# Reordering the FFN products of a hybrid GLA/Fourier block: activations turned among the A products, w_d granules moved, adaLN steps moved

## The chip, the cores and the metric

The kernel runs on one core of a Trainium2 chip. The metric is device time in microseconds (us) of one launch; lower is better. A core has five engines with queues of their own: TensorE (PE in the profile; its weight loads are PEld), VectorE (DVE), ScalarE (ACT), GpSimd (POOL) and SyncE (SP, which here only issues DMAs). Each works through its own queue in order; semaphores make one wait for another. TensorE writes into PSUM, which has eight banks; VectorE and ScalarE read from there.

## The reference, cut to what matters

One layer of a backbone is computed for 128 context tokens and 256 latent tokens, 384 in all, with d_model 2048. The mixing half of the layer (gated linear attention, Fourier branch, gates, output projection) is not touched. What the change touches is the channel half:

```
mod = silu(cond) @ w_ada + b_ada           # six vectors of 2048: shift, scale, gate, twice
h   = rmsnorm(x, norm_pre_ffn) * (1 + sc2) + sh2
ff  = (silu(h @ w_ffn_gate) * (h @ w_ffn_up)) @ w_ffn_down
x   = x + ga2 * rmsnorm(ff, norm_post_ffn)
```

The hidden width is 5632. All arithmetic is float32 in accuracy: each operand is split into a high part (rounded to fp32r) and a low part (the rest), and a product takes three matmuls, high by high, low by high and high by low.

## The kernel before, in words

**Chunks and granules.** The hidden width is cut into NFC = 11 chunks of 512 columns (`FC` = 4 blocks of 128). Chunk 0 is computed plainly. From chunk c = 1 on, chunk c's gate and up products and the down product of chunk c - 1 are interleaved; one such stretch is called stage c here. The weights come in granules of 128 x 1024 float32 (512 KB). A step of the hand-written list `steps` consumes one granule.

**Saved products.** The three 128-token tiles, the halves of the contraction and the gate/up pair are treated with a Strassen-like scheme, so that some products use sums of weights and sums of activations. The kinds of a stage's steps, four steps (i = 0 to 3) of each:

- A (12 matmuls a step), B (12), C (12), E (6), F (6), G (12), H (6): the gate and up products of chunk c. A, B, C and G use loaded granules; the granules of B, E, F and H are formed on VectorE by subtracting others (lines L1412, L1436, L1437, L1439: 128 x 1024 each).
- D with i = 4 to 7 (18 matmuls each): w_d's plain granules, columns 1024 to 2047 of the output, for chunk c - 1. An even i opens three PSUM tiles (`pd_tiles`, pool psm, tag mm), an odd i closes them.
- DA to DH (6 or 12 matmuls): w_d's block products, columns 0 to 1023, by the saving scheme. They use the turned activations (`hid`) and sums of them (`dt["S"]`).

Matmuls of all these have the line L1530 in the profile; the tile name tells them apart: pgu for A to H, pdn for D, pds for DA to DH.

**Splitting.** `grab2` (called at the start of a step) takes the step's split granule, lets loads be issued (`load_more`) and splits the granule three steps ahead (`split_next`): ScalarE copies the high part (L1429, whi), VectorE subtracts to get the low part (L1440, wlo). There are four buffers for each part. Between the two, `split_next` emits up to three operations of the list `pend`, and then the weight sums that this granule needs.

**Turning.** The hidden activations of three token tiles lie as g0, g1, s5 (tokens in rows) and are needed with hidden columns in rows. `turn_hid` makes four transposes on TensorE into a psm bank (tile ptr, L1594) and appends the ScalarE copy and the VectorE subtraction (L1596) to `pend`. In the kernel before this happens after B0, B1 and B2. After B3, `hid_sums` appends seven operations that form `dt["S"]`: they read tiles t = 1 and t = 2 straight out of PSUM (L1604 on ScalarE, two operations at L1605 and two at L1606 on VectorE), and then split the result (L1607). A D step with even i first empties `pend`. The psm pool has three banks, which ptr, pdn, pds and the small reductions share.

**Evictions.** `evict` appends to `pend` what combines the PSUM results at the end of A to H: after E and F an addition and a SiLU, after G two additions and two products (L1583, L1584), after H a product (L1587).

**The last adaLN vector.** ga2 is computed on the side by the generator `ada_last`: 64 steps, each loading 256 KB of w_ada (tile w, two buffers) and running two VectorE operations (L1473; L1471 for the first step of a quarter); after each 16 a small reduction on TensorE (pr, ptm) and three small VectorE operations. `step(ada)` runs it at a rate: before 0.85 per call, called after each A step, each G step, and each D step with i of 4 or more.

**The last stage.** In stage 10 (`LAST` = 10) the down product of chunk 9 is all plain (D0 to D7), and after H follow the rest of them and, after a turn into `hidE`, the eight plain granules of chunk 10.

**Sums in HBM.** Down products of chunks 0 to 8 are staged by ScalarE (`to_sums`, L1632) and added into an HBM array by DMAs from POOL's queue (L1636); the last stage reads them back (`sums_back`, `sums_rest`).

The queues of TensorE, ScalarE, VectorE and GpSimd run in the order in which the code emits (`manual_schedule`); SP's loads are placed by the framework.

Of the kernel before, what the change touches and what calls it, by code (L numbers as in the profile page):

```python
# [96 lines left out]
def tile_step(ctx: ExitStack, tc: tile.TileContext, a, o):  # L97
# [152 lines left out]
    def step(side):  # L250
        if side is not None:
            next(side, None)
# [792 lines left out]
    with ExitStack() as s:  # L1045
# [292 lines left out]
        steps = []  # L1338
        LAST = NFC - 1
        for c in range(1, NFC):  # L1340
            steps += [("A", c, i) for i in range(4)] + [("B", c, i) for i in range(4)]
            if c < LAST:
                dd = iter([("D", c - 1, 4), ("D", c - 1, 5), ("DA", c - 1, 0), ("DB", c - 1, 0), ("DC", c - 1, 0),
                           ("D", c - 1, 6), ("D", c - 1, 7)] + [("D" + k, c - 1, 0) for k in "EFGH"])
            else:
                dd = iter([("D", c - 1, i) for i in range(4)] + [None, ("D", c - 1, 4), None, ("D", c - 1, 5)])
            more = lambda: [x for x in (next(dd, None),) if x]
            for i in range(4):
                steps += [("C", c, i), ("E", c, i)] + more()
            for i in range(4):  # L1350
                steps += [("F", c, i), ("G", c, i)] + more()
            for i in range(4):
                steps += [("H", c, i)] + more()
        steps += [("D", NFC - 2, 6 + i) for i in range(2)]
        d_order = (0, 2, 1, 3)
        steps += [("D", NFC - 1, 2 * n + k) for n in d_order for k in range(2)]

# [281 lines left out]
        def sums_back():  # L1639

            psums.append(actp.tile([P, 6, 512], F32, tag="B_hi", name="psums"))
            w = [adap.tile([P, 2, 512], F32, tag="adaw", name="back", bufs=2) for _ in range(2)]
            at = dict(q2=unit(0, 0), q3=unit(0, 1), p2=unit(1, 0), p3=unit(1, 1), p4=unit(2, 0), p5=unit(2, 1))
            at.update({k: w[n // 2][:, n % 2, :] for n, k in enumerate(("q1", "p1", "p6", "p7"))})
            for k, x in at.items():
                SP.dma_start(x, sums_d[PROD.index(k)])
            return at
# [26 lines left out]
            DVE.tensor_add(u, u, p)  # L1674
            d_live[0] -= 1

        rate[0] = 0.85
        ada = paced(ada_last(), rate)
        pd_tiles, hid_last, x1b, done = None, None, None, 0
        d_bank, hid_pt = {}, []  # L1680
        for kind, c, i in steps:
# [8 lines left out]
            if kind == "D":  # L1690
# [15 lines left out]
                if kh == 1:  # L1706
# [6 lines left out]
                    else:  # L1713
# [5 lines left out]
                        if done == 2:  # L1719
                            pend.append(lambda: DVE.tensor_add(r3, r3, ssq[:, :, 2]))  # L1720
                        done += 1
                if not last_c and i >= 4:
                    step(ada)
                if (c, i) == (NFC - 2, 6):

                    while pend:
# [4 lines left out]
            elif kind[0] == "D":  # L1731
                w = grab2()
                while pend:
                    pend.pop(0)()
                todo = []
                for n, stat, first, last in of_d[kind]():
                    if first:
                        d_bank[n] = psm.tile([P, 512], F32, tag="mm", name="pds")
                        d_live[0] += 1
                    todo.append((d_bank[n], stat, mov_d, first, last))  # L1740
                    if last:
                        pend.append(lambda k=PROD.index(n), p=d_bank[n], c=c: to_sums(k, p, c))
                products(w, todo, by_tile=kind in ("DB", "DC"))
            else:
                w = grab2()
                if kind == "H" and i == 0:
                    while pend:
                        pend.pop(0)()
                B = banks(c)
                products(  # L1750
                    w, [(B[n], two_of(stat, i), mov_gu, first and i == 0, i == 3, not first) for n, stat, first in of_kind[kind]],
                    by_tile=(kind, i) in (("A", 3), ("B", 0), ("B", 3), ("C", 0)),
                )
                if i == 3:
                    evict(c, kind)
                if (kind, c, i) == ("C", LAST, 0):
                    sums_join(back)
                if (kind, c, i) == ("F", LAST, 0):
                    sums_rest()
                if kind == "B":  # L1760
                    if c == 1 and i == 0:
                        d_tiles()
                        load_more()
                    if c == LAST and i == 0:
                        while pend:
                            pend.pop(0)()
                        back = sums_back()
                    if c > 1 and i < 3:
                        pt = turn_hid(hid, i, psm, "mm")
                        hid_pt.append(pt)  # L1770
                    if c < LAST and i == 3:
                        if c == 1:
                            f = dt["full"]
                            pend.append(lambda: DVE.tensor_add(f, hid[0][:, :, P:T].bitcast(F32), hid[1][:, :, P:T].bitcast(F32)))
                            pend.extend(hid_sums(f[:, :, 0:P], f[:, :, P:]))
                        else:
                            pend.extend(hid_sums(*hid_pt[1:]))
                        hid_pt.clear()
                if kind in "AG":
                    step(ada)  # L1780
            if (kind, c, i) == ("D", NFC - 2, 3):
                while pend:
# [153 lines left out]
```

## Time and profile before

| | us |
|---|---|
| median of 3 runs | 1992.55 |
| lowest and highest | 1991.04, 1995.21 |
| the profiled execution: time | 1990.84 |
| the profiled execution: span | 1989.0 |
| TensorE busy | 1947.8 (98%) |
| VectorE busy | 1639.6 (82%) |
| ScalarE busy | 1005.6 (51%) |
| mean granted TensorE clock | 0.996 |

Times in the views are microseconds from the span's start. In a timeline a row is one instruction, or several equal ones in a row (x3): start, busy time, engine, line, operation, tiles as out<-in, and in brackets the idle time of the engine just before and what ended it. Instructions of one engine overlap a little, so the price of one in a full queue is the distance from its start to the next one's. A row of a waits view is: who waited for whom, us in total, times, the longest. A row of a windows view is a stretch, its length, each engine's busy time and instructions, the granted TensorE clock, the DMA engines' share and GB/s. The granted clock tells when TensorE runs at half speed.

### The profile page before, as it was taken

The numbers are of one execution on the slowest core, as the hardware profiler recorded it, in microseconds if no ns is written. First come the engines' busy times: TensorE is split into PE (matmuls) and PEld (weight loads), VectorE is DVE, ScalarE is ACT, GpSimd is POOL, SyncE is SP. The second block draws the span as 40 slices with busy tenths as digits, with TensorE's granted clock in tenths as the row PEclk, the third lists the DMA queues.
The fourth block names the chain that finished last, engine by engine and source line by source line (L and its number), as shares of the span: only waits on it lengthen the run. The fifth ranks groups of instructions, "written<-read, shape, count | busy, mean of one in ns | idle before, by whom it ended". The sixth has DMA issues, their size and how long they took to land.

```text
span 1989.0 us, 28106 instructions
## 1 busy us (share of the span) xinstructions
PE 1947.8 (98%) x10522; PEld 1717.5 (86%) x10522; DVE 1639.6 (82%) x2047; ACT 1005.6 (51%) x1468; POOL 144.4 (7%) x172
## 2 busy tenths in 40 slices
PE   8999999999999999999999999999999999999998
PEld 5779999999999999999987778787878778887876
DVE  5669888888867897968899899979897989887975
ACT  4233554544346654446455555555556555556444
POOL 0000000000000000003000111010102020212001
PEclk9999999999999999999999999999999999999999
DMA  9968677767755786655365768676868595949553
GB/s 390 371 248 272 230 242 245 228 222 251 254 171 167 236 277 225 202 174 207 101 207 195 206 175 226 176 202 170 223 178 205 168 240 153 222 126 222 164 201 113
DMA packets 212457, 422.06 MB, mean 212 GB/s; under 512 B 16732, under 2 KB 115228, under 8 KB 207968
## 3 DMA queue, kind: packets, MB, share of 16 engines
q1 hardware_dynamic: 193744, 386.31, 57.7%
q0 software_dynamic: 18432, 33.56, 10.9%
q8 instruction: 82, 1.34, 0.3%
q14 instruction: 55, 0.45, 0.1%
q10 hardware_dynamic: 144, 0.39, 0.1%
HBM read 365.68 MB, written 54.53 MB: 211 GB/s over the span
## 4 chain that ended last, share of the span: by engine, by line
PE 74%; DVE 12%; DMA 7%; issue 4%; ACT 2%; SPq 0%; POOL 0%; DVEq 0%; ACTq 0%; POOLq 0%
PE pmm L258 34%; PE pgu L1530 16%; PE pdn L1530 8%; DVE wlo L1440 5%; PE pds L1530 4%; PE pv L398 3%; DVE acc L1473 2%; DMA raw<-in_w_u 1%; PE pgm L381 1%; DMA raw<-in_w_g 1%; ACT whi L1429 1%; DMA raw<-in_w_d 1%; DMA slab<-in_w_ada 1%; PE pf L996 1%; PE px L416 1%
## 5 line engine op out<-in xcount | busy, mean ns | idle before, releaser
L258 PE MATMUL pmm<-A_hi,whi 128*128 128x384 f32 x1200 | 404.3, 337 | 0.0
L258 PE MATMUL pmm<-A_hi,wlo 128*128 128x384 f32 x1200 | 401.4, 334 | 0.0
L258 PE MATMUL pmm<-A_lo,whi 128*128 128x384 f32 x1200 | 401.3, 334 | 0.0
L1429 ACT CAST whi<-u 128x1024 fp32r<-128x1024 f32 x200 | 208.9, 1054 | 172.2 <-DVE u L1412 69.1
L224 ACT CAST whi<-raw 128x1024 fp32r<-128x1024 f32 x181 | 189.8, 1051 | 177.4 <-DMA raw<-in_w_gate 61.2
L1429 ACT CAST whi<-raw 128x1024 fp32r<-128x1024 f32 x157 | 165.0, 1051 | 206.7 <-DMA raw<-in_w_u 61.8
L225 DVE TENSOR_TENSOR wlo<-raw,whi 128x1024 fp32r<-128x1024 f32 x179 | 218.0, 1221 | 55.8 <-ACT whi L224 54.2
L1530 PE MATMUL pgu<-whi,A_hi 128*128 128x512 f32 x640 | 250.3, 391 | 2.0 <-ACT whi L1429 1.7
L1440 DVE TENSOR_TENSOR wlo<-u,whi 128x1024 fp32r<-128x1024 f32 x200 | 241.5, 1219 | 12.7 <-ACT whi L1429 11.1
L1530 PE MATMUL pgu<-whi,A_lo 128*128 128x512 f32 x640 | 249.3, 389 | 0.0
L258 PEld LDWEIGHTS pmm<-A_hi,whi 128*128 128x128 f32 x1200 | 225.3, 188 | 2.9 <-issue 1.8
L1440 DVE TENSOR_TENSOR wlo<-raw,whi 128x1024 fp32r<-128x1024 f32 x157 | 191.7, 1221 | 42.5 <-ACT whi L1429 38.0
L258 PEld LDWEIGHTS pmm<-A_lo,whi 128*128 128x128 f32 x1200 | 225.3, 188 | 0.2
L258 PEld LDWEIGHTS pmm<-A_hi,wlo 128*128 128x128 f32 x1200 | 225.2, 188 | 0.0
L572 DVE SCALAR_TENSOR_TENSOR adacc<-adaw,spad,adacc 128x1024 f32<-128x1024 f32 x180 | 222.8, 1279 | 2.1 <-DMA adaw<-in_w_ada 1.9
L1530 PE MATMUL pgu<-wlo,A_hi 128*128 128x512 f32 x640 | 186.9, 391 | 6.6 <-DVE wlo L1440 6.5
L1530 PEld LDWEIGHTS pgu<-wlo,A_hi 128*128 128x128 f32 x640 | 120.0, 188 | 33.7 <-DVE wlo L1440 8.7
L1530 PEld LDWEIGHTS pgu<-whi,A_hi 128*128 128x128 f32 x640 | 120.3, 188 | 29.7 <-ACT whi L1429 2.1
L1530 PEld LDWEIGHTS pgu<-whi,A_lo 128*128 128x128 f32 x640 | 120.2, 188 | 25.0
L1530 PE MATMUL pgu<-whi,S 128*128 128x512 f32 x400 | 119.5, 396 | 0.0
L1530 PE MATMUL pdn<-whi,hid_hi 128*128 128x512 f32 x264 | 104.7, 397 | 12.3 <-DVE dw L1606 12.2
L1636 POOL DMA_DIRECT2D sums_d<-spare x64 | 58.7, 992 | 664.6 <-ACT spare L1632 474.8
(401 smaller groups left out, 3286.0 us busy)
## 6 DMA issues: line engine op xcount, KB each, us to landing
adaw<-in_w_ada SPq DMA_DIRECT2D x96, 512.0 KB, 4.2
raw<-in_w_d SPq DMA_DIRECT2D x70, 512.0 KB, 4.0
slab<-in_w_ada SPq DMA_DIRECT2D x32, 1024.0 KB
raw<-in_w_gate SPq DMA_DIRECT2D x64, 512.0 KB, 4.6
raw<-in_w_g SPq DMA_DIRECT2D x48, 512.0 KB, 3.9
raw<-in_w_u SPq DMA_DIRECT2D x48, 512.0 KB, 5.1
raw<-in_w_in SPq DMA_DIRECT2D x44, 512.0 KB, 4.5
u<-in_w_u SPq DMA_DIRECT2D x40, 512.0 KB, 5.3
```

The lines of the kernel that those rows point to most:

```text
L224: ACT.copy(hi, raw)
L225: sub = lambda: eng.tensor_sub(lo, raw, hi.bitcast(F32))
L258: PE.matmul(dst, w[wi][:, k * n + n0 : k * n + n0 + P], x[xi][:, k0 + k, :], start=first and k == 0 and j == 0, stop=last and k == kts - 1 ...
L381: PE.matmul(pgv[q : q + 32, :], spad[:, k, :], slab[k // (KT // 2)][:, k % (KT // 2), :], start=k < 4, stop=k >= KT - 4,)
L398: PE.matmul(pv[2 * t + g], hT[x_][:, kb, t * P : (t + 1) * P], w_[:, g * 512 : (g + 1) * 512], start=kb == 0 and j == 0, stop=kb == KT - 1 ...
L416: PE.matmul(px, w_[:, u * P : (u + 1) * P], hT[x_][:, kb, :], start=j == 0, stop=j == 2)
L572: DVE.scalar_tensor_tensor(acc[:, c, :], w, spad[:, k, c : c + 1], acc[:, c, :], op0=ALU.mult, op1=ALU.add,)
L1429: ACT.copy(hi, src)
L1440: DVE.tensor_sub(lo, src, hi.bitcast(F32))
L1473: DVE.scalar_tensor_tensor(acc[:, c, :], w, spad[:, k, c : c + 1], acc[:, c, :], op0=ALU.mult, op1=ALU.add,)
L1530: PE.matmul(dst, stat[x_][m], mov(w[w_], m), start=first and w_ == m == x_ == 0, stop=last and w_ == m == 1, skip_group_check=any(more),)
L1636: POOL.dma_start(sums_d[k], u, accum_op=ALU.add)
```

## The change

The order of steps within a stage is written anew, the turns and the adaLN steps move with it; no instruction is added or taken away.

- Order of w_d's products in stages 1 to 9. Before: after E0 D4, after E1 D5, after E2 DA, after E3 DB, after G0 DC, after G1 D6, after G2 D7, after G3 DE, after H0 DF, after H1 DG, after H2 DH. After: after B1 D4, after E0 D5, after E1 DA, after E2 DB, after E3 DC, after G0 D6, after G1 D7, after G2 DE, after G3 DF, after H1 DG, after H2 DH.
- Stage 10. Before: D0 to D3 after E0 to E3, D4 after G1, D5 after G3, D6 and D7 after H. After: D0 to D3 the same, D4 after G3, D5 to D7 after H.
- The turns of tiles 0, 1, 2 stand after A1, A2, A3 instead of B0, B1, B2; `hid_sums` is appended after A3 instead of B3; in stage 1 `d_tiles()` comes after A2 instead of B0, with `pend` emptied ahead of it.
- `step(ada)` is called after A and B steps instead of A, G and D (i of 4 or more), at a rate of 1.0 instead of 0.85.

```diff
--- before.py
+++ after.py
@@ -1338,20 +1338,21 @@
         steps = []
         LAST = NFC - 1
         for c in range(1, NFC):
-            steps += [("A", c, i) for i in range(4)] + [("B", c, i) for i in range(4)]
+            d = c - 1
             if c < LAST:
-                dd = iter([("D", c - 1, 4), ("D", c - 1, 5), ("DA", c - 1, 0), ("DB", c - 1, 0), ("DC", c - 1, 0),
-                           ("D", c - 1, 6), ("D", c - 1, 7)] + [("D" + k, c - 1, 0) for k in "EFGH"])
+                after = {("B", 1): 4, ("E", 0): 5, ("E", 1): "DA", ("E", 2): "DB", ("E", 3): "DC", ("G", 0): 6, ("G", 1): 7}
+                after.update({("G", 2): "DE", ("G", 3): "DF", ("H", 1): "DG", ("H", 2): "DH"})
             else:
-                dd = iter([("D", c - 1, i) for i in range(4)] + [None, ("D", c - 1, 4), None, ("D", c - 1, 5)])
-            more = lambda: [x for x in (next(dd, None),) if x]
-            for i in range(4):
-                steps += [("C", c, i), ("E", c, i)] + more()
-            for i in range(4):
-                steps += [("F", c, i), ("G", c, i)] + more()
-            for i in range(4):
-                steps += [("H", c, i)] + more()
-        steps += [("D", NFC - 2, 6 + i) for i in range(2)]
+                after = {("E", i): i for i in range(4)}
+                after["G", 3] = 4
+            for kinds in ("A", "B", "CE", "FG", "H"):
+                for i in range(4):
+                    for k in kinds:
+                        steps.append((k, c, i))
+                        x = after.get((k, i))
+                        if x is not None:
+                            steps.append(("D", d, x) if isinstance(x, int) else (x, d, 0))
+        steps += [("D", NFC - 2, 5 + i) for i in range(3)]
         d_order = (0, 2, 1, 3)
         steps += [("D", NFC - 1, 2 * n + k) for n in d_order for k in range(2)]
 
@@ -1674,7 +1675,7 @@
             DVE.tensor_add(u, u, p)
             d_live[0] -= 1
 
-        rate[0] = 0.85
+        rate[0] = 1.0
         ada = paced(ada_last(), rate)
         pd_tiles, hid_last, x1b, done = None, None, None, 0
         d_bank, hid_pt = {}, []
@@ -1719,8 +1720,6 @@
                         if done == 2:
                             pend.append(lambda: DVE.tensor_add(r3, r3, ssq[:, :, 2]))
                         done += 1
-                if not last_c and i >= 4:
-                    step(ada)
                 if (c, i) == (NFC - 2, 6):
 
                     while pend:
@@ -1757,17 +1756,18 @@
                     sums_join(back)
                 if (kind, c, i) == ("F", LAST, 0):
                     sums_rest()
-                if kind == "B":
-                    if c == 1 and i == 0:
+                if (kind, c, i) == ("B", LAST, 0):
+                    while pend:
+                        pend.pop(0)()
+                    back = sums_back()
+                if kind == "A" and i:
+                    if c == 1 and i == 2:
+                        while pend:
+                            pend.pop(0)()
                         d_tiles()
                         load_more()
-                    if c == LAST and i == 0:
-                        while pend:
-                            pend.pop(0)()
-                        back = sums_back()
-                    if c > 1 and i < 3:
-                        pt = turn_hid(hid, i, psm, "mm")
-                        hid_pt.append(pt)
+                    if c > 1:
+                        hid_pt.append(turn_hid(hid, i - 1, psm, "mm"))
                     if c < LAST and i == 3:
                         if c == 1:
                             f = dt["full"]
@@ -1775,8 +1775,9 @@
                             pend.extend(hid_sums(f[:, :, 0:P], f[:, :, P:]))
                         else:
                             pend.extend(hid_sums(*hid_pt[1:]))
+                    if i == 3:
                         hid_pt.clear()
-                if kind in "AG":
+                if kind in "AB":
                     step(ada)
             if (kind, c, i) == ("D", NFC - 2, 3):
                 while pend:
```

## The prediction

> **What bounds the kernel now.** I read the page first, then the busy time of the ten FFN stages (one per hidden chunk, between the starts of their A products), then who TensorE waits for in them, and last the order of VectorE's work in one stage.
>
> ```profile
> span 1989.0 us, 28106 instructions
> PE 1947.8 (98%) x10522; PEld 1717.5 (86%) x10522; DVE 1639.6 (82%) x2047; ACT 1005.6 (51%) x1468; POOL 144.4 (7%) x172
> ```
> ```profile
> 1161.00:1256.40 95.40, 93.64 (x415) 76.31 (x414) 89.74 (x95) 53.55 (x68) 14.00 (x16) 1.00 0.77 204
> 1256.40:1355.20 98.80, 95.95 (x432) 77.92 (x432) 84.98 (x90) 54.10 (x70) 13.99 (x16) 0.98 0.71 188
> ```
> ```profile
> PE pdn L1530 <- DVE dw L1606: 12.2, 7, 2.8
> PE pgu L1530 <- DVE wlo L1440: 6.5, 4, 3.0
> PE pdn L1530 <- DVE hidE L1596: 2.6, 1, 2.6
> PE pgu L1530 <- ACT whi L1429: 1.7, 1, 1.7
> PE pds L1530 <- DVE wlo L1440: 0.9, 3, 0.3
> ```
> TensorE is the bound. Of a stage of 95 to 99 us it is busy 94 to 96 us and VectorE 85 to 90 us, so VectorE is nearly full too. The third block is nearly all that TensorE waits for in ten stages: some 24 us. Half is the first w_d product of a stage, step D4 (i = 4, pdn), waiting for the hid_sums subtraction of L1606, which reads the turned activations out of PSUM and so holds the last of the three banks that D4 needs. No edit adds or removes an instruction: the same products, splits and loads run in another order. So the sum is one of waits, and it is made in stage 4:
>
> ```profile
> 1256.45 0.39 PE L1530 MATMUL pgu<-whi,A_hi 128*128 128x512 f32 x1
> ...
> 1270.20 0.60 PE L1594 MATMUL ptr<-ident,ep 128*128 128x128 f32 x4
> 1270.55 0.71 PE L1530 MATMUL pgu<-whi,S 128*128 128x512 f32 x2
> ...
> 1285.48 0.39 PE L1530 MATMUL pdn<-whi,hid_lo 128*128 128x512 f32 x1
> 1288.63 0.53 PE L1530 MATMUL pdn<-whi,hid_hi 128*128 128x512 f32 x1 [2.76 <-DVE dw L1606]
> 1288.96 0.62 PE L1530 MATMUL pdn<-whi,hid_lo 128*128 128x512 f32 x1
> ```
> ```profile
> 1194.40 4.08 PE pgu L1530 x18
> ```
> ```profile
> 1288.90:1292.40 3.50, 3.50 (x10) 2.69 (x10) 3.50 (x4) 2.23 (x3) 0.00 (x0) 0.51 0.50 150
> ```
> Unhindered, 18 matmuls take 4.08 us (from the chain), 0.227 each; twelve, a step of A or B, take 2.72. A turn (four transposes) puts the next product off by 0.35 between the starts shown, and some 0.1 more within it. D4's ninth matmul, the first into the third bank, waits 2.76 us, and then TensorE runs 3.4 us at a granted clock of 0.51, which costs 1.7 us more.
>
> ```profile
> 1254.60 3.49 DVE L1440 TENSOR_TENSOR wlo<-u,whi 128x1024 fp32r<-128x1024 f32 x3
> 1258.00 0.68 DVE L1587 TENSOR_TENSOR ep<-ep,pgu 128x512 f32<-128x512 f32 x1
> 1258.60 1.22 DVE L1412 TENSOR_TENSOR u<-u,u 128x1024 f32<-128x1024 f32 x1
> 1259.74 1.22 DVE L1440 TENSOR_TENSOR wlo<-u,whi 128x1024 fp32r<-128x1024 f32 x1
> 1260.87 1.41 DVE L1473 SCALAR_TENSOR_TENSOR acc<-w,spad,acc 128x512 f32<-128x512 f32 x2
> 1262.20 1.22 DVE L1412 TENSOR_TENSOR u<-u,u 128x1024 f32<-128x1024 f32 x1
> ...
> 1278.13 0.68 DVE L1596 TENSOR_TENSOR hid_lo<-ptr,hid_hi 128x512 fp32r<-128x512 f32 x1
> 1278.73 1.21 DVE L1440 TENSOR_TENSOR wlo<-u,whi 128x1024 fp32r<-128x1024 f32 x1
> ...
> 1283.62 0.88 DVE L1605 TENSOR_TENSOR dw<-dw,ptr 128x256 f32<-128x256 f32 x2 [1.95 <-ACT dw L1604]
> 1284.42 1.22 DVE L1436 TENSOR_TENSOR u<-raw,u 128x1024 f32<-128x1024 f32 x1
> ...
> 1287.83 0.75 DVE L1606 TENSOR_TENSOR dw<-ptr,dw 128x256 f32<-128x256 f32 x2
> ```
> VectorE's price is the distance between starts: 1.14 for a 1024-wide subtraction (L1412, L1440), 1.33 for one ada step (the pair at L1473), 0.60 for a turn's low part or the H product (L1587), 0.80 for the pair at L1605; the pair at L1606 is done after 0.75. All of it is in order: a wait of this queue delays everything behind it.
>
> **The change part by part.**
>
> *D4 behind B1, turns among A, hid_sums after A3, ada in A and B.* These belong together, for all set when VectorE comes to the last L1606. Count from the start of A0. VectorE begins the H product at 1258.00 - 1256.45 = 1.55 (the splits before it wait for the weight buffers that the last H steps free, so relief in H can bring this forward by some 0.3 only). By the new order of the code there follow, ahead of the last L1606: the H product 0.60; four L1412 4.55; six low parts (A3, B0, B1, D4, B2, B3; splits run three steps ahead) 6.8; three turns 1.8; the two L1605 0.8; the two L1606 to their end 0.75; and ada steps at A0 to A3, B0, B1: six, 8.0 (the four A steps at the rate of 0.85 gave 3.4). Sum 1.55 + 23.3 = 24.8. TensorE needs it earlier: six steps of A and B 16.3, three turns 1.4, eight matmuls of D4 1.8: 19.5, where before two more B steps, C0 and E0 lay ahead. The wait is 5.3 us, and with the half clock (1.7 at most, 1.6 taken, for the clock's drop falls partly in the wait) 6.9. Without ada the same sum gives 16.8 and no wait, so ada's move carries it.
>
> By code, stages 2, 4, 6 and 8 have six ada steps there: 27.6. In stages 3, 5 and 7 a quarter of ada ends in A: one step less, one cheaper (0.88 for the pair at L1471, below, against 1.41), TensorE itself later by the quarter's reduction (an estimate of 0.8): wait 3.2 and half clock 1.6, together 14.4. In stage 9 three steps are left: about 1. Sum 43. Before: 12.2 idle, 0.16 more in each of 8 stages (a matmul's modelled end lies that far behind its successor's start) and two half clocks: 17. Difference **+26**. Bounds: -17, if the wait vanishes; +38, if in eight stages VectorE also waits 1.5 us for its ada rows.
>
> ```profile
> w<-in_w_ada SPq DMA_DIRECT2D x64, 256.0 KB, 5.0
> sums_d<-dw POOLq DMA_DIRECT2D x64, 256.0 KB, 7.7
> ```
> ```profile
>   DMA w<-in_w_ada: 2.5, 2
> ```
> Two buffers hold those rows; a load starts when the step two before is done. With 3.5 us from step to step that leaves 5.9 us for 5.0, so it is hidden by 0.9. On SP's queue the w_d load of D5 comes between them, which waits for D4's low part; that ends before the ada step that frees the next buffer, so nothing is held up. On POOL's queue nothing changes its order, but hid_sums overwrites the staging tile (dw) from which the H products' sums go out around A0: with 7.7 to landing it is free some 5 us before the copy after A3 writes it.
>
> *Stage 1.*
> ```profile
> 975.10 1.22 DVE L1440 TENSOR_TENSOR wlo<-u,whi 128x1024 fp32r<-128x1024 f32 x1
> ...
> 978.51 0.88 DVE L1471 TENSOR_SCALAR acc<-w,spad 128x512 f32<-128x512 f32 x2
> ```
> ```profile
> 969.59 0.39 PE L1530 MATMUL pgu<-whi,A_hi 128*128 128x512 f32 x1
> ```
> Here A3's low part starts 5.5 us after A0 (969.59), against 3.3 in stage 4, for the last left sum stands ahead of it. D4 does not wait for the sums, but two more ada steps and D4's and the sums' operations come ahead of C0's low part: it would end near 31 where TensorE needs it near 28. With a half clock and less what waits there now: **+4** (0 to 8).
>
> *w_d's other products one place earlier, ada gone from G and D.*
> ```profile
> 1242.80 1.22 DVE L1440 TENSOR_TENSOR wlo<-dw,whi 128x1024 fp32r<-128x1024 f32 x1
> 1243.93 1.41 DVE L1473 SCALAR_TENSOR_TENSOR acc<-w,spad,acc 128x512 f32<-128x512 f32 x2
> 1245.26 0.68 DVE L1583 TENSOR_TENSOR ep<-ep,pgu 128x512 f32<-128x512 f32 x1
> ...
> 1247.18 1.22 DVE L1440 TENSOR_TENSOR wlo<-u,whi 128x1024 fp32r<-128x1024 f32 x1
> ```
> Now H1's low part stands behind an ada step and the G evictions (stage 3), which gives the pgu waits for wlo of L1440. In the new order H1 is split ahead of the G evictions, and no ada step is there. DG's low part then ends about 4.5 us after G3, and TensorE needs it 26 matmuls after G3: 5.9. So these waits go: 6.5, less 1.1 in another place, pds waits of 0.9, 0.16 for each of some dozen waits, and the half clock after the 3.0: **-10** (-11 to -5). In C3, E3, DC VectorE now has seven 1024-wide operations (8.0) against 30 matmuls (6.8); in C0 to C2 it gains as much beforehand (5.7 to 6.8 against 6.8 to 8.2), so I take nothing.
>
> *The end.* D0 of the last chunk waits for hidE:
> ```profile
> 1935.51 1.04 ACT L1429 CAST whi<-raw 128x1024 fp32r<-128x1024 f32 x1 [4.36 <-DMA raw<-in_w_d]
> 1936.46 1.55 ACT L1596 CAST hidE<-ptr 128x512 fp32r<-128x512 f32 x3
> ```
> ScalarE's copies of hidE stand behind a cast that waits for a w_d load. With D5 behind H, one product more (4.08 us) lies between that load's issue and its need: of 2.6 and a half clock about 1.7 stays: **-2.6** (-4.3 to 0). The pgu wait of 1.7 for ACT (stage 9, a load behind the sums read back) may go: **-1** (-2 to 0).
>
> Sum: 26 + 4 - 10 - 2.6 - 1 = +16.4. Against the profiled execution (span 1989.0, time 1990.84) that is 2007.2; the median of the runs, 1992.55, is 1.7 higher, so I predict **2009 us**.
>
> The Trainium skill (TensorE: Matmul & The Clock Gate, section Part 1) says that the array falls to half rate after at least one idle window of about 3.4 us. This trace halves after 2.76 us, so it disagrees at the edge. By that rule the waits of 3.2 us would not be followed by a half clock.
>
> **The rivals.**
>
> *Faster: VectorE reaches the last L1606 before D4's third bank is wanted.* It decides in A0 to B1: if VectorE's work there fits into 18 us instead of 23.3, all of the 17 goes, and 10 and 3.6 besides: 1992.55 - 31 = 1962. Break-even is a D4 cost of about 3.3 us per stage with the half clock. For it speaks that turns and sums start two to three steps earlier, against it that VectorE is busy without a gap from 1254.60 on and that ada steps are put just there. 0.15.
>
> *Ada rows come late.* The margin of 0.9 us is small; if each of the six steps loses 0.3 to 0.5, a stage loses 2 to 3 more and the time is 1992.55 + 16 + 20 = 2029 at most, 2024 in the middle. Against it: VectorE now idles 2.5 us in all for these rows (last row above). 0.13.
>
> *No half clock after waits just over 3 us.* Stages 3, 5 and 7 lose 1.6 less each: 2004. The pauses of 2.76 and 3.0 speak against it. 0.05. That is what the page's rule would give.
>
> *The moves cancel.* D4 costs 3.3 per stage instead of 5 to 7, for instance because quarter ends and turns leave more room: 1993, within 0.2%. 0.05.
>
> **How the numbers follow.** The forecast has 0.62. 0.2% (4 us) is about what a measurement of this kernel can tell from no change. Faster 0.15, same 0.05, slower 0.80. The range of 8 in 10 goes from 1993 (the moves cancel) to 2024 (late ada rows); the forecast's own, from its terms' bounds, is 1999 to 2019.
>
> **What would show it.** In the new trace, D4 of stages 2 to 8 waits 4.5 to 6 us for the last hid_sums subtraction (L1607 there) at its ninth matmul, with the clock near 0.5 for 3.4 us after it; VectorE is without a gap from the H product to that subtraction; H1 and DG wait for nothing. I am wrong if D4 starts without a wait, if VectorE idles for ada rows, or if the waits move into B2, C or F.

## The result

| | before | after |
|---|---|---|
| median of 7 runs, us | 1992.59 | 1999.14 |
| lowest and highest, us | 1986.56, 1995.21 | 1998.51, 2001.36 |
| profiled execution: time, us | 1990.84 | 2001.36 |
| mean granted TensorE clock | 0.996 | 0.993 |

The change makes the kernel slower: the ratio is 1.0036, with a 95% interval of 1.0023 to 1.0048, that is 6.5 us of medians, where 16.4 were forecast. The direction was forecast, the amount two and a half times too large. The page of the kernel after begins with these lines (its lines behind the edits are numbered one higher than before: L1441 is before's L1440, L1531 is L1530, L1607 is L1606):

```profile
span 1999.6 us, 28113 instructions
PE 1951.4 (98%) x10522; PEld 1722.9 (86%) x10522; DVE 1644.5 (82%) x2047; ACT 1014.0 (51%) x1468; POOL 144.4 (7%) x172
```

What TensorE waits for from the first FFN stage on (who waits for whom, us, times, longest):

```profile
PE pdn L1531 <- DVE dw L1607: 18.2, 8, 2.5
PE pdn L1531 <- DVE dw L1606: 7.4, 6, 1.6
PE pgu L1531 <- DVE wlo L1441: 3.8, 2, 2.9
...
PE pdn L1531 <- DVE hidE L1597: 1.4, 2, 0.9
```

D4's waits for the sums have grown from 12.2 to 25.6 us; the waits of H1 and DG for a low part (6.5) are gone, and the 3.8 that now stand in that row lie in stage 1. Stage 4 of the kernel after, VectorE's and TensorE's rows from its timeline; A0 starts at 1265.95:

```profile
1266.57 0.68 DVE L1588 TENSOR_TENSOR ep<-ep,pgu 128x512 f32<-128x512 f32 x1
...
1284.47 1.42 DVE L1474 SCALAR_TENSOR_TENSOR acc<-w,spad,acc 128x512 f32<-128x512 f32 x2
1285.80 0.88 DVE L1606 TENSOR_TENSOR dw<-dw,ptr 128x256 f32<-128x256 f32 x2
1286.71 0.42 DVE L1607 TENSOR_TENSOR dw<-ptr,dw 128x256 f32<-128x256 f32 x1
1287.05 1.22 DVE L1441 TENSOR_TENSOR wlo<-u,whi 128x1024 fp32r<-128x1024 f32 x1
1288.18 1.41 DVE L1474 SCALAR_TENSOR_TENSOR acc<-w,spad,acc 128x512 f32<-128x512 f32 x2
1289.51 0.42 DVE L1607 TENSOR_TENSOR dw<-ptr,dw 128x256 f32<-128x256 f32 x1
```
```profile
1283.73 0.39 PE L1531 MATMUL pdn<-whi,hid_hi 128*128 128x512 f32 x1
...
1286.37 0.47 PE L1531 MATMUL pdn<-whi,hid_hi 128*128 128x512 f32 x1 [1.57 <-DVE dw L1606]
...
1289.98 0.50 PE L1531 MATMUL pdn<-whi,hid_hi 128*128 128x512 f32 x1 [2.46 <-DVE dw L1607]
```
```profile
1265.95:1364.71 98.76, 94.73 (x415) 77.63 (x414) 87.87 (x91) 54.91 (x68) 14.01 (x16) 0.98 0.73 193
...
1289.90:1293.40 3.50, 3.42 (x9) 2.75 (x10) 2.39 (x4) 1.05 (x1) 0.00 (x0) 0.60 0.24 80
```

The last subtraction ends at 1289.93, 24.0 us after A0 (24.8 were forecast), with a split's low part and the sixth ada step between the two L1607. D4 waits twice, for its second bank and for its third, and runs its next 3.5 us at a granted clock of 0.60.

Where the time went, counted from the starts of all FFN matmuls in the two profiled executions (all that lies beyond 0.2266 us from one start to the next; the sum is 57.5 us before and 67.4 after):

| part | before | after | difference | forecast |
|---|---|---|---|---|
| D4 and the half clock right behind it, stages 2 to 9 | 17.9 | 39.7 | +21.8 | +26 |
| stage 1 without its H steps | 1.9 | 7.2 | +5.3 | +4 |
| H0 to DH | 11.9 | 0 | -11.9 | -10 |
| G1 of stage 9 | 2.0 | 0 | -2.0 | -1 |
| D0 of the last chunk | 4.3 | 2.0 | -2.3 | -2.6 |
| turns, ada's small reductions, the rest | 19.5 | 18.5 | -1.0 | 0 |

### The profile page after: what moved, and what is told of

The parts are those of the page before. It is cut to its first block, busy times and chain, and to the rows that moved or that the text cites. A ratio compares the mean times of both kernels' runs of the same rounds, so it can differ in the third digit from the quotient of the medians.

```text
span 1999.6 us, 28113 instructions
## 1 busy us (share of the span) xinstructions
PE 1951.4 (98%) x10522; PEld 1722.9 (86%) x10522; DVE 1644.5 (82%) x2047; ACT 1014.0 (51%) x1468; POOL 144.4 (7%) x172
## 4 chain that ended last, share of the span: by engine, by line
PE 85%; DVE 9%; DMA 2%; issue 2%; ACT 2%; SPq 0%; POOL 0%; DVEq 0%; ACTq 0%; POOLq 0%
PE pmm L258 34%; PE pgu L1531 24%; PE pdn L1531 10%; PE pds L1531 6%; PE pv L398 3%; DVE wlo L1441 3%; DVE acc L1474 2%; DVE u L1413 1%; PE pgm L381 1%; DMA slab<-in_w_ada 1%; PE pf L996 1%; PE px L416 1%; PE pmm L1251 1%; DMA raw<-in_w_d 1%; PE po L645 0%
## 5 line engine op out<-in xcount | busy, mean ns | idle before, releaser
L1441 DVE TENSOR_TENSOR wlo<-u,whi 128x1024 fp32r<-128x1024 f32 x200 | 242.8, 1222 | 29.7 <-PE pdn L1531 14.5
L1531 PE MATMUL pgu<-whi,A_hi 128*128 128x512 f32 x640 | 251.2, 392 | 0.0
L1531 PE MATMUL pgu<-whi,A_lo 128*128 128x512 f32 x640 | 249.4, 390 | 0.0
L1441 DVE TENSOR_TENSOR wlo<-raw,whi 128x1024 fp32r<-128x1024 f32 x157 | 191.9, 1222 | 34.8 <-ACT whi L1430 31.9
L1531 PE MATMUL pgu<-wlo,A_hi 128*128 128x512 f32 x640 | 186.5, 390 | 2.9 <-DVE wlo L1441 2.9
L1531 PEld LDWEIGHTS pgu<-wlo,A_hi 128*128 128x128 f32 x640 | 120.3, 188 | 28.6 <-DVE wlo L1441 3.3
L1531 PEld LDWEIGHTS pgu<-whi,A_hi 128*128 128x128 f32 x640 | 120.2, 188 | 25.1 <-issue 0.6
L1531 PEld LDWEIGHTS pgu<-whi,A_lo 128*128 128x128 f32 x640 | 120.2, 188 | 24.6
L1531 PE MATMUL pdn<-whi,hid_hi 128*128 128x512 f32 x264 | 105.7, 400 | 25.7 <-DVE dw L1607 18.2
L1531 PE MATMUL pgu<-whi,S 128*128 128x512 f32 x400 | 119.9, 398 | 0.0
```

The costliest lines, as they stand in the source:

```text
L1441: DVE.tensor_sub(lo, src, hi.bitcast(F32))
L1531: PE.matmul(dst, stat[x_][m], mov(w[w_], m), start=first and w_ == m == x_ == 0, stop=last and w_ == m == 1, skip_group_check=any(more),)
```

## The experiments

All ratios are to the kernel before, measured beside each run. Times are medians. A product "loses" the time between the starts of its matmuls beyond 0.2266 us each, as in the table above.

| run | what | us | ratio [95%] |
|---|---|---|---|
| ada_back | after, ada in A, G, D again | 1982.36 | 0.9959 [0.9944, 0.9973] |
| d4_back | after, w_d's order of before | 2006.16 | 1.0076 [1.0061, 1.0091] |
| turns_only | before, turns and sums among A | 1991.64 | 0.9998 [0.9987, 1.0010] |
| fill | after, 16 matmuls more in each D4 | 1992.35 | 1.0007 [0.9998, 1.0017] |
| ada_only | before, ada in A and B | 2020.68 | 1.0145 [1.0125, 1.0166] |
| left_later | d4_back, the split into left behind B3 | 1989.48 | 0.9983 [0.9969, 0.9996] |
| turns_left | turns_only, the split into left behind B3 | 1997.83 | 1.0026 [1.0014, 1.0038] |
| left_f | left_later, stage 1's ada moved to F0 | 1989.41 | 0.9986 [0.9975, 0.9996] |
| by_bank | after, D4 bank by bank | 1985.65 | 0.9968 [0.9955, 0.9980] |
| spread | after, ada at A0 and from F0 to F2 | 2004.42 | 1.0065 [1.0050, 1.0080] |
| spread_e | spread, E0 in place of F2 | 1975.81 | 0.9923 [0.9908, 0.9937] |
| spaced2 | after, ada at A0, A1, B2, B3, F0, D6, G1, D7 | 1958.72 | 0.9831 [0.9813, 0.9848] |

### Is it ada, D4's place, or the turns? Four runs

**ada_back.** The theory: ada's six steps ahead of the last subtraction carry D4's wait. The rival: D4 behind B1 costs by itself.

```diff
-        rate[0] = 1.0
+        rate[0] = 0.85
@@ behind products of a D step
+                if not last_c and i >= 4:
+                    step(ada)
@@ behind the gate and up steps
-                if kind in "AB":
+                if kind in "AG":
                     step(ada)
```

> The changed kernel with its ada steps where they were before (after A and G steps and after D4 to D7, at a rate of 0.85). Theory (ada's move carries D4's wait): in stage 4 of the changed kernel VectorE reaches the end of the last hid_sums subtraction 24.0 us after A0, 0.6 of it before the H product and 8.0 for six ada steps. With 3.4 steps there, 4.5 us, it ends near 20.5 to 21.1, where TensorE wants it at 19.6: D4 loses 1 to 2 us a stage instead of 4.8 (38.0 us in eight stages, by the starts of its matmuls), and the half clock behind it is gone. The waits before H1 and DG, 11.9 us before the change, stay away if the new order of w_d's products removed them, and come back if ada's leaving G and D did. Time: 1999 - 38 + 12 = 1973, or 1985 with all H waits back. Rival (D4's place behind B1 costs by itself, whatever VectorE has to do): D4 still loses 4 us or more a stage, 1993 or more.

Measured: 1982.36. TensorE's waits from the first FFN stage on:

```profile
PE pdn L1531 <- DVE dw L1607: 7.7, 7, 1.1
PE pdn L1531 <- DVE dw L1606: 5.8, 6, 1.8
PE pds L1531 <- DVE wlo L1441: 4.6, 3, 1.8
```

D4's idle time falls from 25.6 to 13.5 us and what it loses in all from 38.0 to 22.0: more than expected, because the chain starts 1.5 us later again (the H product stands 2.1 us behind A0 in most stages, where it is 0.62 in the kernel after). DE to DH, the stretch around H, lose 11.4 us, against 12.4 in the kernel before: these waits are back although the new order of products stands. So ada's leaving G and D removed them, not the new order. The time lies where the theory put it.

**d4_back.** The steps list of before in the kernel after, nothing else.

```diff
-                after = {("B", 1): 4, ("E", 0): 5, ("E", 1): "DA", ("E", 2): "DB", ("E", 3): "DC", ("G", 0): 6, ("G", 1): 7}
-                after.update({("G", 2): "DE", ("G", 3): "DF", ("H", 1): "DG", ("H", 2): "DH"})
...
+                dd = iter([("D", c - 1, 4), ("D", c - 1, 5), ("DA", c - 1, 0), ("DB", c - 1, 0), ("DC", c - 1, 0),
+                           ("D", c - 1, 6), ("D", c - 1, 7)] + [("D" + k, c - 1, 0) for k in "EFGH"])
```

> The changed kernel with the w_d products in their old order (D4 behind E0); turns and sums stay among A, ada stays in A and B. Theory (VectorE's chain against TensorE's need): the last hid_sums subtraction still ends some 24 us after A0, but D4's ninth matmul now comes after two more B steps, C0 and E0: 19.6 + 9.5 = 29.1. No wait in D4, no half clock there: 38 us less. The H waits: none if ada's leaving G removed them, up to 12 us if the order did. Time 1961 to 1973. Rival (VectorE, 85 to 90 us busy in a stage of 98, is so full that the wait only moves to C and E): some 2 to 4 us a stage return there, 1980 to 1992.

Measured: 2006.16. A miss of 33 us or more. The H waits are gone as expected (H0 to DH lose 0.1 us), and D4 waits for nothing, but C0 does. TensorE's waits, and stage 4's timeline:

```profile
PE pgu L1530 <- ACT ep L1573: 22.8, 8, 3.4
PE pgu L1530 <- DVE wlo L1440: 4.2, 5, 2.7
PE pgu L1530 <- ACT whi L1429: 3.5, 1, 3.5
```
```profile
1290.59 0.41 DVE L1606 TENSOR_TENSOR dw<-ptr,dw 128x256 f32<-128x256 f32 x1
...
1291.03 1.04 ACT L1607 CAST left<-dw 128x1024 fp32r<-128x1024 f32 x1 [2.80 <-DVE dw L1606]
1291.98 1.04 ACT L1429 CAST whi<-raw 128x1024 fp32r<-128x1024 f32 x1
...
1292.93 0.58 ACT L1573 COPY ep<-pgu 128x512 f32<-128x512 f32 x1
...
1293.56 0.66 PE L1530 MATMUL pgu<-whi,S 128*128 128x512 f32 x1 [3.43 <-ACT ep L1573]
```

The last operations of hid_sums are ScalarE's cast into left and VectorE's subtraction. ScalarE's cast waits for VectorE's last subtraction; behind it in ScalarE's queue stands the copy of B's bank Z (L1573), and C0 writes into that bank next. So the chain on VectorE is a gate even where D4 is not behind it: C0 and E0 lose 41.8 us in this run.

**turns_only.** The kernel before with its `turn_hid` and `hid_sums` calls moved as in the change.

```diff
-                if kind == "B":
+                if kind == "A" and i:
...
-                    if c > 1 and i < 3:
-                        pt = turn_hid(hid, i, psm, "mm")
+                    if c > 1:
+                        hid_pt.append(turn_hid(hid, i - 1, psm, "mm"))
```

> The kernel before with one part of the change alone: turns among A, hid_sums after A3. Order of products and ada steps as before. Theory: VectorE's chain to the last hid_sums subtraction was 29 to 32 us after A0 because the third turn's low part was 22 us after A0; with the turns four steps earlier it ends near 22, and D4 wants it at 29. The 17.6 us that D4 loses go, the H waits (11.9 us) stay: 1992.6 - 17.6 = 1975. Rival (hid_sums come earlier but D4's bank was late for another reason, or the sums now delay the splits of B): 1985 to 1995.

Measured: 1991.64, no change. D4's 17.6 us are gone (0.6 left), and C0 and E0 lose 18.6 instead, by the same copy on ScalarE:

```profile
PE pgu L1530 <- ACT ep L1573: 11.4, 8, 2.1
PE pgu L1530 <- DVE wlo L1440: 6.3, 4, 2.5
```
 The last subtraction does come earlier (24.5 us after A0 in stage 4 instead of 32.1, for 22 expected); that this would be a gain was wrong: the wait has moved.

**ada_only.** The kernel before with only ada's calls in A and B.

```diff
-        rate[0] = 0.85
+        rate[0] = 1.0
...
-                if not last_c and i >= 4:
-                    step(ada)
...
-                if kind in "AG":
+                if kind in "AB":
                     step(ada)
```

> The kernel before with one part of the change alone: ada steps after A and B at a rate of 1.0; turns among B, D4 behind E0. Theory: VectorE's chain to the last hid_sums subtraction, 32.1 us after A0 in stage 4 of the kernel before, gets 4.6 steps of 1.33 more and starts 0.9 earlier, so it ends near 36 where D4 wants it at 29: 7 us and a half clock of 1.6 in each of stages 2, 4, 6 and 8, a little less in 3, 5 and 7, against 17.6 in all before, and H's 11.9 go: 1991 + 58 - 17.6 - 11.9 = 2020. Rival (ada's place does not matter to D4): 1980, H's waits alone gone.

Measured: 2020.68.

```profile
PE pdn L1530 <- DVE dw L1606: 21.6, 7, 3.3
PE pdn L1530 <- DVE dw L1605: 8.7, 6, 2.7
```

In stage 4 the last subtraction ends 34.4 us after A0 (36 was worked out), D4 loses 46.5 us in all, and H0 to DH are down to 0.9. Of the change's parts this is the one that costs. The earlier turns take back some 14 us of it (d4_back, 2006.16), and the new order of products some 7 more (the kernel after, 1999.14). The new order was not run without the turns.

### What the half clock costs

**fill.** The waits of D4 stay, but TensorE is kept busy in them with products into a bank that is not in use.

```diff
             for at, (ws, (dst, stat, mov, first, last, *more)) in enumerate(order):
+                for _ in range(fill.get(at, 0)):
+                    PE.matmul(pgu[0], stat[0][0], mov(w[0], 0), start=True, stop=True)
...
-                products(w, todo, by_tile=last_c and kh == 1)
+                products(w, todo, by_tile=last_c and kh == 1, fill={1: 6, 2: 10} if i == 4 and c < LAST - 1 else {})
```

> The changed kernel with 16 matmuls more in each of the eight D4 steps behind B1 (6 before the second bank's first matmul, 10 before the third's; they write a bank that nobody reads). They take 16 x 0.227 = 3.6 us of time in which TensorE waits: 1.7 and 2.6 us in stage 4. Theory (six of the eight waits put TensorE at half clock for 3.4 us, 1.6 us each): with the array kept busy the clock stays, 9 us less; they overfill the waits of stages 7 and 9 by some 3 us: 1999 - 9 + 3 = 1993, and in the trace no granted clock near 0.5 in D4. Rival (the clock falls for another reason than the pause, or costs nothing): 1999 + 3 = 2002.

Measured: 1992.35, 6.8 us less than the kernel after (1993 was expected). The mean granted clock rises from 0.993 to 0.999; the stretch around D4 of stage 4:

```profile
1264.00:1290.00 26.00, 25.63 (x118) 20.63 (x117) 24.82 (x32) 11.81 (x15) 0.00 (x0) 1.00 0.33 100
```

So the clock falls because of the pauses, and more work on TensorE makes the kernel faster. The half clock costs the kernel after at least these 6.8 us. In the profiled executions D4 of stages 2 to 9 with the half clock behind it loses 33.2 us instead of 39.7, the unused matmuls counted as loss; stage 1, whose D4 the edit fills too, loses 4.4 instead of 7.2.

### Can the wait be paid elsewhere?

**left_later.** In d4_back the first five operations of hid_sums stay behind A3, the two of left go behind B3's eviction, so that ScalarE's copy of Z is ahead of them.

```diff
-                            pend.extend(hid_sums(*hid_pt[1:]))
+                            sums = hid_sums(*hid_pt[1:])
+                        pend.extend(sums[:5])
+                if kind == "B" and i == 3 and c < LAST:
+                    pend.extend(sums[5:])
```

> D4 back behind E0 as in d4_back, and of hid_sums only the five operations that read the banks follow A3; its split into left (ScalarE's cast and VectorE's subtraction, L1607 of d4_back) follows B3, behind ScalarE's copy of B's sum. Theory (in d4_back the wait sat at C0 because ScalarE's copy of bank Z, L1573, stood in its queue behind the cast of left at 1291.0, which waits for VectorE's last hid_sums subtraction, while the matmuls that need the bank came at 1290): the copy is free as soon as B3 is done, and the 36 us that C0 and E0 lose in stages 2 to 9 go. Last subtraction 24 to 26 us after A0, D4 wants it at 29. Time 2006 - 36 = 1970, waits in H none. Rival (VectorE is too full, and whatever stands behind its chain waits): some 3 us a stage come back at D4 or in C and E, 1990 or more.

Measured: 1989.48, against 2006.16 for d4_back: ScalarE's copy is confirmed as that run's gate, but only 17 of 36 us stay gained. The rest is in C now:

```profile
PE pgu L1530 <- DVE wlo L1440: 19.5, 14, 2.7
PE pdn L1530 <- DVE hidE L1596: 3.0, 2, 2.5
```

C0 and C1, which wait for their low parts, lose 22.5 us. In stage 6 VectorE works without a gap from A0 to 38.9 us behind it, past the start of C1 (33.0), and whatever stands late in that stretch is late for TensorE. The rival was right: it put the time at 1990 or more.

**turns_left** does the same to turns_only. **left_f** takes ada out of A and B in stage 1 of left_later, for one step after F0 of each stage:

```diff
-                if kind in "AB":
+                if (kind in "AB" and c > 1) or (kind, i) == ("F", 0):
                     step(ada)
```

> Turns and sums among A in the kernel before, as in turns_only, with the split into left behind B3. Theory: the 13.5 us that C0 and E0 lost in stages 2 to 9 of turns_only go, D4 still loses nothing; the H waits (10.9 us) and G1 of stage 9 (4.6 us) stay: 1991.6 - 13.5 = 1978. Rival: the wait comes back at D4, 1990.

> left_later with no ada step in stage 1's A and B; one step after F0 of every stage takes their place. Theory: stage 1 loses 8.6 us in d4_back because two more ada steps stand ahead of C0's low part; 6 to 8 of these go, and F0, where VectorE has room (no split for the next product but 1.14 of 4.1 us), takes the step without a wait: 1963. Rival (stage 1's loss comes from the full sum of hid and the sums' operations, which stay): as left_later, 1970.

Measured: 1997.83 and 1989.41, both misses. In turns_left C0's loss of 13 us goes as in left_later, but C1 loses 12.2 (0 in turns_only), C3 3.5 (0), D6 7.7 (3.4) and H0 to DG 17.0 (10.9); in sum it is some 6 us worse than turns_only. The waits have moved once more. In left_f stage 1 loses 0.5 us instead of 6.6, but the shifted rhythm puts four of ada's reductions (pr) into B, where TensorE comes to them before VectorE has made their sums:

```profile
PE pr L1482 <- DVE acc L1473: 11.1, 4, 5.7
```

**by_bank.** In the kernel after, D4 alone does its three banks one after the other, so that the third is wanted at the thirteenth matmul instead of the ninth.

```diff
-                products(w, todo, by_tile=last_c and kh == 1)
+                products(w, todo, by_tile=last_c and kh == 1 or i == 4 and c < LAST - 1)
```

> The changed kernel with D4's 18 matmuls bank after bank (six into the first, six into the second, six into the third), where they were twelve with the high part and then six with the low part. Theory: the second bank is wanted two matmuls later and the third four later, 0.9 us, so of D4's waits in stages 2 to 9 0.9 each goes, 7 in all, and pauses that fall below some 2.6 us cost no half clock: 1999 - 7 - (0 to 5) = 1987 to 1992. Rival (the low part of D4 is itself late, or VectorE's chain follows TensorE's): 1996 to 1999.

Measured: 1985.65, 1.4 us below the range of the theory. D4 and the half clock in B2 lose 29.3 us instead of 39.7. That is 10.4, where the later need of the banks accounts for 8 x 0.9 = 7; I take the rest for half clock, as the theory had it, but did not measure it by itself.

### Ada where VectorE has room

**spread** and **spread_e.** The kernel after, its eight ada steps a stage at named places.

```diff
-                if kind in "AB":
-                    step(ada)
+            if (kind, i) in SITES:
+                step(ada)
```

In spread SITES is A0, F0, G0, D6, F1, G1, D7, F2; in spread_e it is A0, E0, F0, G0, D6, F1, G1, D7.

> The changed kernel's order of products, turns and sums; its eight ada steps a stage follow A0, F0, G0, D6, F1, G1, D7 and F2 (rate 1.0) and none the other A and the B. Theory (what VectorE has to do between the H product and the last hid_sums subtraction sets D4's wait, and ada between D4 and the last H split sets H's): one ada step in place of six takes 6.7 us from the chain: 24.0 - 6.7 = 17.3 after A0, before D4's third bank is wanted at 19.6, so D4's 38.0 us go. Behind D4, the seven steps take 9.3 us of VectorE between F0 and F2, where TensorE has 84 matmuls or 19 us and VectorE 10.2 of splits: no wait, and none ahead of H1, for the G evictions are three steps later. Time 1999 - 38 = 1961, stage 1 perhaps 5 less. Rival (the waits move again, as they moved to C0 and C1 in d4_back and left_later): 4 us a stage come back in C or H, 1985.

> As spread, with one step after E0 in place of F2. Theory: behind E0 VectorE has D5's split alone against 36 matmuls of C1, E1 and D5, so this costs nothing, and G2's split is 1.3 us earlier: as spread, 1961. Rival: C2 and C3, where VectorE is fullest (3.4 us for a C, 2.3 for DA and DC), inherit the 1.3 us: 1961 + 8 = 1969 or more.

Measured: 2004.42 and 1975.81. Both lie above the theory (1961). spread also lies above its rival (1985); spread_e lies in its rival's range (1969 or more), but C2 and C3, which the rival named, lose nothing. In both D4's loss is 0.4 us a stage: with one ada step ahead of it the last subtraction is in time. Here ada's place alone takes 35 us from D4, which settles the cause of D4's wait. One step in F2 instead of E0 costs 29 us. VectorE's waits in spread, and three rows of its stage 4:

```profile
DVE acc L1474 <- DMA w<-in_w_ada: 45.4, 15, 4.7
```
```profile
1327.06 1.41 DVE L1474 SCALAR_TENSOR_TENSOR acc<-w,spad,acc 128x512 f32<-128x512 f32 x2
1328.38 1.22 DVE L1441 TENSOR_TENSOR wlo<-raw,whi 128x1024 fp32r<-128x1024 f32 x1
1332.72 1.42 DVE L1474 SCALAR_TENSOR_TENSOR acc<-w,spad,acc 128x512 f32<-128x512 f32 x2 [3.12 <-DMA w<-in_w_ada]
```

VectorE stands still for a load of 256 KB, and the splits behind it with it: G3 loses 33.7 us in this run. The same view of spread_e has 24.0 us in 8 waits. This is the rival of the late ada rows, in a place where the prediction did not look for it. In the kernel after VectorE waits for these rows not once.

**spaced2.** The steps further apart; in stage 1 they follow A0, E0, F0, G0, D6, G1 and D7. A form without any ada step in A and B of stage 1 (spaced) came to a deadlock and has no time.

```diff
+        late = {("F", 0), ("D", 6), ("G", 1), ("D", 7)}
+        sites = {("A", 0), ("A", 1), ("B", 2), ("B", 3)} | late, {("A", 0), ("E", 0), ("G", 0)} | late
-                if kind in "AB":
-                    step(ada)
+            if (kind, i) in sites[c == 1]:
+                step(ada)
```

> The changed kernel's order, with the eight ada steps of stages 2 to 10 after A0, A1, B2, B3, F0, D6, G1 and D7, and the seven of stage 1 after A0, E0, F0, G0, D6, G1 and D7. Theory: two ada steps ahead of the last hid_sums subtraction in place of six take 5.3 us from the chain, 24.0 - 5.3 = 18.7 after A0 against TensorE's 19.6, so D4 loses about 0.4 a stage as in spread_e; between F0 and D7 one step comes to 18 matmuls or more, 4 us, so that ada's rows (two buffers) are not late as they were in spread (45.4 us of VectorE's waits) and spread_e (24.0), and the 20 us that spread_e lost at G2, DE, F3, H0 and DG go; B2 and B3 stand behind the subtraction, where the changed kernel had steps as well without a loss at C0. Time 1976 - 20 = 1956. Rival (VectorE's two steps in B2 and B3 come back at C1 and C3, as in left_later): 1.5 to 2 us a stage, 1968 to 1972.

Measured: 1958.72, as worked out within 3 us, and 1.7% faster than the kernel before. TensorE's largest waits from the first FFN stage on:

```profile
PE py L1819 <- DVE psums L1808: 1.6, 1, 1.6
PE pdn L1531 <- DVE hidE L1597: 1.2, 2, 0.6
PE pdn L1531 <- DVE dw L1607: 1.0, 2, 0.5
```

Its matmuls lose 26.2 us where those of the kernel after lose 67.4; 13.2 of it are the turns, which every version has. Six ada steps ahead of the last subtraction are too many, two fit.

## Why the prediction was right in direction and wrong in size

- **D4 waits for the last hid_sums subtraction, and ada's move carries it.** Right, by name: the wait, its place, the order on VectorE and the six ada steps are in the trace, and ada_only (+28 us alone), ada_back and spread_e show the cause. VectorE is gapless but for 0.07 us between the H product and the last subtraction of stage 4.
- **The failed step: the start of VectorE's chain.** The sum began with the H product at 1.55 us after A0 and allowed relief in H to bring this forward by "some 0.3 only", because the splits before it were taken to wait for weight buffers that TensorE frees. It is 0.62 in all of stages 2 to 9, 0.93 earlier. In the kernel before, at the H product of stages 2 to 7, those splits did not wait for TensorE. ScalarE's last wait ahead of them was for a sum of VectorE (3.38 us in stage 4), and VectorE itself ran without a gap for the 12 us up to the H product: it was late. In the kernel after VectorE has caught up: ScalarE's last wait there, in all eight stages, is one of 0.2 us for TensorE. The rows are one of ScalarE and one of VectorE before, then one of ScalarE after:

```profile
1250.25 1.05 ACT L1429 CAST whi<-dw 128x1024 fp32r<-128x1024 f32 x1 [3.38 <-DVE dw L1439]
...
1253.46 4.62 DVE L1440 TENSOR_TENSOR wlo<-u,whi 128x1024 fp32r<-128x1024 f32 x4
```
```profile
1264.34 1.05 ACT L1430 CAST whi<-u 128x1024 fp32r<-128x1024 f32 x1 [0.20 <-PE pds L1531]
```

What made VectorE late in the kernel before were mainly ada's steps in G and D: with ada alone moved (ada_only) the H product stands at 0.62 in six of the eight stages, with ada left or put back there (turns_only, ada_back) at 1.5 and 2.1 in six. They are not the only thing that can: in left_later, without them, it is 1.5 in six stages. A wait of TensorE in H does not by itself delay the start: of the kernel before, H of stage 7 loses the most (H1 3.5 us, DG 1.2), and the H product behind it stands at 0.69.
- **What the step was worth.** The rest of the chain was 23.3 by the sum and 23.4 in the trace. In the even stages D4 loses 6.2 us with its half clock (6.9 forecast), in stages 3, 5 and 7 13.4 together (14.4), in stage 9 1.6 (1). The term came to +21.8 instead of +26: 3.3 us less in the new waits, and 0.9 because the old ones lose 17.9 where the sum had 17. Ada's move was priced only as work put into A and B; it also took work off VectorE's queue ahead of the chain, which moved the whole chain forward.
- **The wait at the ninth matmul only.** Wrong in part: 7.4 of the 25.6 us of waits are at the fifth, for the second bank, in six stages. In stage 4 the two are 1.57 and 2.46, where one of 4.5 to 6 was named as the sign. The sum goes by the last subtraction alone and is hardly touched.
- **H1 and DG wait for nothing.** Right, -11.9 us against -10. But of the two reasons given, the place of H1's split and ada's absence, ada_back and d4_back show that the second does it.
- **Stage 1, the end, stage 9.** +5.3 for +4, -2.3 for -2.6, -2.0 for -1. Stage 1's loss is ada as well: spaced2, with one step in its A and none in its B, loses 0.1 us there.
- **The cover that was taken for granted.** I took nothing for C0 to C3. That holds in the kernel after only because TensorE waits at D4 first: d4_back and left_later show that C0 and C1 would have waited next, for ScalarE's copy and for VectorE. The rival "faster" put 31 us of gain on the condition that VectorE's work ahead of D4 fits. Where less work makes it fit, the gain is there (spaced2: 34.6 us); where D4 is moved out of the way of the same work (d4_back), it is not.
- **What is left.** The terms measure +9.9, and the profiled executions differ by 10.5 us, not 16.4. Of the 6.5 us between the terms and their forecast, 4.2 are D4's, 1.9 H's; the others nearly cancel. The medians differ by 6.5: the profiled execution of before lies 1.75 below its median, that of after 2.2 above. These 4 us are no part of any term. What makes executions of before differ by 9 us (1986.56 to 1995.21) and those of after by 3 was not tried.
- **Of the rivals** neither late ada rows nor a gain by the earlier sums came about here. The third, no half clock behind pauses of 3.2 us, has a part of the truth: in stage 7, where the wait came out at 2.52 us, the clock stayed at 1.00, and in six other stages it fell. No length of a pause decides it by itself, as the last section shows.

## What to carry to other kernels

A wait at the end of a queue belongs to the queue's whole length: before moving work, add up what the engine has to do between its last gate and the next, and count work that the same change takes off the queue ahead of that gate as an earlier start of the sum. Taking one wait away (D4 moved in d4_back, the sums earlier in turns_only) is worth nothing as long as the engine is full there; the wait goes to the next reader, even by way of a third engine's queue. What pays is to move side work into the stretch where the engine has room, and with a distance that its loads can keep.

## What the runs showed of the hardware

The clock can fall after several short pauses, not only after one long. In ada_back, stage 4, TensorE pauses for 1.76 us, runs four matmuls, pauses for 1.12 us, and then runs at a granted clock of 0.55; in the kernel after, stage 7, one pause of 2.52 us was followed by 1.00.

```profile
1274.74 0.47 PE L1531 MATMUL pdn<-whi,hid_hi 128*128 128x512 f32 x1 [1.76 <-DVE dw L1606]
...
1277.03 0.62 PE L1531 MATMUL pdn<-whi,hid_hi 128*128 128x512 f32 x1 [1.12 <-DVE dw L1607]
```
```profile
1276.90:1280.40 3.50, 3.37 (x8) 2.63 (x9) 2.38 (x4) 1.05 (x1) 0.00 (x0) 0.55 0.00 0
```
```profile
1585.48 0.50 PE L1531 MATMUL pdn<-whi,hid_hi 128*128 128x512 f32 x1 [2.52 <-DVE dw L1607]
```
```profile
1584.50:1587.90 3.40, 2.42 (x10) 1.99 (x11) 2.29 (x4) 1.05 (x1) 0.00 (x0) 1.00 0.26 77
1587.90:1591.30 3.40, 3.40 (x16) 2.82 (x15) 3.40 (x4) 2.02 (x2) 0.00 (x0) 1.00 0.02 5
```

The length of a single pause does not decide it either. In turns_only two pauses of 2.11 us, with no other pause over 0.3 us within 5 us of them, were followed by 0.71 and by 1.00. In turns_left one of 1.82 us was followed by 0.54, in d4_back one of 3.02 us by 1.00.

```profile
1284.23 0.50 PE L1530 MATMUL pgu<-whi,S 128*128 128x512 f32 x1 [2.11 <-ACT ep L1573]
...
1382.47 0.50 PE L1530 MATMUL pgu<-whi,S 128*128 128x512 f32 x1 [2.11 <-ACT ep L1573]
```
```profile
1284.20:1287.60 3.40, 3.37 (x11) 2.68 (x12) 3.40 (x4) 1.12 (x2) 0.00 (x0) 0.71 0.13 22
1382.50:1385.90 3.40, 3.40 (x15) 2.82 (x16) 3.40 (x4) 1.19 (x2) 0.00 (x0) 1.00 0.04 13
```

The Trainium skill (TensorE: Matmul & The Clock Gate, Part 1) says that the gate watches a free-running window of about 3.4 us, and that the array goes to half rate after at least one idle window. That the window is free-running agrees with pauses of like length that do and don't lower the clock; that the window must be idle as a whole does not agree with 1.76 and 1.12 us of pause with matmuls between.
